# Half of a branch's gated product kept on chip, loads issued in another order, a smaller DMA scratch

## The chip, the cores and the metric

The program runs on one core of a Trainium2 chip. The core has a matrix engine (TensorE, PE in the profile; its weight loads are PEld), a vector engine (VectorE, DVE), a scalar engine (ScalarE, ACT), a general engine (GpSimd, POOL) and a sync engine (SyncE, SP) that issues transfers. Each engine takes its own instructions in order and waits on semaphores for the others; transfers run on 16 DMA engines. The metric is the device time of one execution, in microseconds, and the median of several executions.

## What is computed

A bidirectional encoder of two layers on one sequence of 512 tokens with 1024 channels, in float32. Cut to what matters:

```python
for l in range(DEPTH):                                   # DEPTH = 2
    xn = rms_norm(x, ln1[l])
    z = xn @ w_in[l]                                     # one projection for all branches
    a_q, a_i, a_ff, a_fb, a_g, b_u, b_v, c_q, c_k, c_v, gz = jnp.split(z, offsets, axis=-1)
    o_a = hgrn2_bidirectional(a_q, a_i, a_ff, a_fb, lower[l])         # branch A, 4 heads
    y_a = rms_norm(o_a, a_norm[l]) * jax.nn.silu(a_g)
    y_b = spatial_gating(jax.nn.gelu(b_u), jax.nn.gelu(b_v), w_s[l], b_s[l])
    y_c = window_attention(rope(c_q), rope(c_k), c_v, sink[l])        # branch C, 8 query heads
    gates = jax.nn.sigmoid(gz.reshape(bsz, s_len, N_BRANCH, D_MODEL))
    merged = (gates[:, :, 0] * (y_a @ w_br[l, 0])
              + gates[:, :, 1] * (y_b @ w_br[l, 1])
              + gates[:, :, 2] * (y_c @ w_br[l, 2]))
    x = x + merged @ w_out[l]
    x = x + jnp.square(jax.nn.relu(rms_norm(x, ln2[l]) @ w_up[l])) @ w_down[l]
return rms_norm(x, final_norm)
```

The change touches the last of the three products in `merged` and what follows it up to the residual.

## The kernel before

**Tiles and precision.** Activations are held as tiles of 128 partitions by 512 values (256 KB). A float32 product is made of three matmuls in a reduced format: every operand is split in a high part (a cast on ScalarE, L207 for weights, L270 for activations) and a low part (a subtraction on VectorE, L208 and L271), and the matmuls are high by high, high by low, and low by high. `proj_tok` (L262 to L264) does this for the projections of the branches with tokens on the partitions: four PSUM tiles, one for each 128 tokens, and half of the 1024 output channels at a time (`fl` is 0 or 1). Weights come through SyncE's queue into `wr` and are split into `wh` and `wl`.

**Order.** The code is written layer by layer. A scheduler puts the instructions of each engine in an order, from the code, its priorities (`later(...)` pushes work back, `hp()` brings it forward) and its own estimate of durations. Tiles come from tags with a fixed number of slots (the table SLOTS); a new tile of a tag waits until the users of the slot's earlier tile are done. At run time each engine keeps its order.

**Stages of a layer around the change.** Branch A's heads run one after the other in `a_head` (L581 to L669). The end of a head is a chain: scores `at` (TensorE, from `qt` and `kt` made by ScalarE), transposes `kT` and their copy (L624, L626), states `stp` and `st` (L629, L636), the product `av` (L652), squares and sums `asq` (ScalarE, L657), `ms` and `rs` (VectorE and GpSimd, L280, L282), the scaled `ao` (VectorE, L660) and transposes `oT` (TensorE, L664). Between its steps stands other work: branch C's attention (scores L972, transposed weights `pT` L1001 and their copy L1002, output `po` L1006, copies to `yc` L1008) and branch C's projection `yC`.

Branch C's gated product (L1054 to L1063): for each half, `gates` loads four tiles `th` from DRAM (tag `ch` here), `yC` is projected, VectorE forms (th + 1) * yC in place, and the tile is stored to the DRAM buffer `mcd`. Both halves go there. Then branch A's four outputs are gated and split into `yh` and `yl` (L1066 and `split`); `yh` takes tag `tv`. That tag has eight slots: earlier in the layer they hold branch A's four value tiles `vt`, branch C's keys `k2` and the low parts of the keys `kl` (two each).

The merge (L1090 to L1106): for each half, loads of `th` and of the four `mC` tiles back from `mcd` (tag `mg`), the projection `yA`, VectorE's (th + 1) * yA at L1101 and the sum into `mC` at L1102. `turn_sum` transposes `mC` to `mT` on TensorE (L1081), loads branch B's part `mB` from DRAM (`mgd`), adds (L1086) and splits the result into `mgh` and `mgl`, the operands of the output projection `wo`. The PSUM tag of the first half's `mT` has two buffers. Then the residual `xr` is loaded (eight tiles, tag `l`, L1111), and `wo` is projected and added to it (L1117).

All loads and stores named here are issued by GpSimd, in its order; an issue waits until the GpSimd transfer eight before it has landed, since their semaphores are used in turn. In layer 0 that order is: eight stores to `mcd`, four `xr`, four `th`, four `mC`, four `mB`, four `mC`, then the other `xr` mixed with the second half's `th`, and the second half's `mB`.

Of the kernel before, what the change touches and what calls it, by code (L numbers as in the profile page):

```python
# [6 lines left out]
F32 = mybir.dt.float32  # L7
# [3 lines left out]
ALU = mybir.AluOpType  # L11

P = 128
S = 512
# [46 lines left out]
def trunk(tc, xT, xt, ws, vec, fnb, bsb, snk, wst, rope, cmask, amask, ident, out):  # L61
    nc = tc.nc
# [3 lines left out]
    def pool(**kw):  # L66
        p = tc.tile_pool(**kw)
        pools.append(p)
        return p.__enter__()
# [6 lines left out]
    dram = pool(name="dram", bufs=1, space=bass.MemoryType.DRAM)  # L76
# [4 lines left out]
             "xs": 16, "zt": 6,  # L81
             "yh": 8,
             "q": 2, "a": 3, "g": 2, "ch": 10,
             "yi": 16, "th": 8, "mg": 8,
             "h": 22}

    HOME = {t: p for p, ts in {"G": ("xs", "zt"), "Y1": ("yh",), "br": ("q", "a", "g", "ch"), "Y2": ("yi", "th", "mg"), "mlp": ("h",)}.items() for t in ts}
# [5 lines left out]
    def nm(s):  # L93
        ctr[0] += 1
        return f"{s}_{ctr[0]}"

    def T(tag, name, dt=F32):
        where = part[HOME[tag]] if tag in HOME else sb
        return where.tile([P, S], dt, tag=tag, bufs=SLOTS[tag], name=nm(name))
# [33 lines left out]
    def hp():  # L133

        return tc.high_priority() if boost[0] else contextlib.nullcontext()
# [562 lines left out]
    for i in range(8):  # L698
        t = T("tv", "xt")
# [5 lines left out]
    xsrc = xt  # L705
    xspill = dram.tile([P, 4, D], F32, name="xspill")
    thd = dram.tile([P, 8, D], F32, name="thd")
    mgd = dram.tile([P, KT, S], F32, name="mgd")
    mcd = dram.tile([P, 8, S], F32, name="mcd")

    for l in range(DEPTH):
        xs = n1.xs
# [176 lines left out]
        def y_split(ys, tag):  # L889
            res = []  # L890
            for y in ys:
                hi, lo = T(tag, "yh", F32R), T(tag, "yl", F32R)
                split(y, hi, lo)
                res.append((hi, lo))
            return res
# [19 lines left out]
        def gate_a():  # L915
            z = evac(proj(xs, "ag", l, "ag", len(sg)), "l2", "ag")
            th = T("jk", "th")
            nc.scalar.activation(th, z, AF.Tanh, scale=0.5)
            nc.vector.scalar_tensor_tensor(z, th, 1.0, z, ALU.add, ALU.mult)
            sg.append(z)  # L920
# [131 lines left out]
        with later(30000):  # L1052
            for h in range(4):
                gate_a()  # L1054

            ys = y_split(yc, "yh")
            for fl in range(2):
                th = gates("ch", 0, fl)
                pts = proj_tok(ys, "yC", (l, "y", 2, fl), 0)
                for t in range(4):  # L1060
                    with hp():
                        nc.vector.scalar_tensor_tensor(th[t], th[t], 1.0, pts[t], ALU.add, ALU.mult)
                    nc.gpsimd.dma_start(mcd[:, fl * 4 + t], th[t])  # L1063
        ys = []
        for h in range(4):
            nc.vector.scalar_tensor_tensor(oa[h], oa[h], 0.5, sg[h], ALU.mult, ALU.mult)  # L1066
# [23 lines left out]
        ms = [None] * KT  # L1090
        for fl in range(2):
            th = gates("th", 1, fl)
            mc = []
            for t in range(4):
                m = T("mg", "mC")
                nc.gpsimd.dma_start(m, mcd[:, fl * 4 + t])
                mc.append(m)
            pts = proj_tok(ys, "yA", (l, "y", 0, fl), fl)
            for t in range(4):
                with hp():  # L1100
                    nc.vector.scalar_tensor_tensor(th[t], th[t], 1.0, pts[t], ALU.add, ALU.mult)  # L1101
                    nc.vector.tensor_tensor(mc[t], mc[t], th[t], ALU.add)  # L1102
            mcs.append(mc)
            if fl == 0:
                turn_sum(0)


        xr = [[T("l", "xr"), T("l", "xr")] for _ in range(4)]
        for fl in range(2):
            for t in range(4):  # L1110
                nc.gpsimd.dma_start(xr[t][fl], xsrc[:, t, fl * S:(fl + 1) * S])  # L1111
        n2 = norm_tok("ln2", l, xr, False)
        for fl in range(2):
            pts = proj_tok(ms, "wo", (l, "wo", fl), fl, None if fl else lambda: turn_sum(1))
# [103 lines left out]
        xsrc = xspill  # L1218
# [121 lines left out]
```

## Time and profile before

| | before |
|---|---|
| runs, us | 1723.64, 1722.11, 1719.17; median 1722.11 |
| profiled execution, us | 1720.54, of which the recorded span is 1718.7 |
| mean granted TensorE clock | 0.997 |
| DMA moved | 200.04 MB, mean 116 GB/s |
| transfers issued by GpSimd | 166 of 256 KB or less |

The profiled execution lies 1.57 us below the median of the runs and 1.84 us above its span. The table of granted clock by slices holds a 9 throughout, so the clock is the same in all stages. In the rows of the trace the first number is the start in us from the span's start, the second the duration in us, then engine, line, operation, output and inputs; brackets hold the idle time of the engine before the row and what ended it. A matmul's recorded duration overlaps the next one: what a train of them costs is read from the distance of their starts.

### The profile page before, as it was taken

The page shows a single profiled execution, that of the slowest core. Times are in us where ns is not written, and L with a number is a line of the kernel's source. Part 1 is how long each engine was busy: PE and PEld are TensorE (multiplying, and loading weights), DVE is VectorE, ACT ScalarE, POOL GpSimd, SP SyncE. Part 2 cuts the span into 40 slices and gives each one's busy share as a digit, 9 for nine tenths or more (in the row PEclk, how much of TensorE's full clock was granted, in tenths as well). Part 3 has the DMA queues.
Part 4 walks back from the last instruction along what each step waited for, and adds up shares of the span by engine and source line. Part 5 has one row for each costly group of instructions (what it writes and reads, how often), then busy time and mean ns, then how long its engine had stood idle before and what let it go on. Part 6 is the DMA issues. An engine that isn't in the chain of part 4 may idle for free.

```text
span 1718.7 us, 21970 instructions
## 1 busy us (share of the span) xinstructions
PE 1679.9 (98%) x8024; PEld 1402.0 (82%) x8024; DVE 1296.1 (75%) x2009; ACT 1016.7 (59%) x1715; POOL 146.3 (9%) x215
## 2 busy tenths in 40 slices
PE   8999989999999999999999999999999999999997
PEld 7888878888778888888888787888878788888886
DVE  7996977687566768686889869876875667585967
ACT  7665567676335555545665754877872355545464
POOL 0011200000310000000010112000004000000001
PEclk9999999999999999999999999999999999999999
DMA  8342232231555332322323422322316453232311
GB/s 333 98 147 92 84 105 75 80 105 55 189 204 183 104 105 98 98 98 98 135 88 127 153 91 74 104 69 86 104 56 246 158 184 99 98 103 94 123 62 49
DMA packets 58283, 200.04 MB, mean 116 GB/s; under 512 B 7904, under 2 KB 8288, under 8 KB 58176
## 3 DMA queue, kind: packets, MB, share of 16 engines
q1 hardware_dynamic: 44640, 154.72, 26.8%
q0 software_dynamic: 13248, 43.40, 6.8%
q8 instruction: 63, 1.03, 0.2%
q10 hardware_dynamic: 288, 0.52, 0.1%
q14 instruction: 44, 0.36, 0.1%
HBM read 177.64 MB, written 20.97 MB: 116 GB/s over the span
## 4 chain that ended last, share of the span: by engine, by line
PE 61%; issue 25%; DVE 8%; ACT 4%; POOL 1%; DMA 1%; POOLq 0%; SPq 0%; DVEq 0%; ACTq 0%
PE up L212 3%; PE up L214 3%; PE up L213 3%; PE at L567 2%; PE dA L427 2%; PE dA L429 2%; PE wo L264 2%; PE dA L428 2%; PE wo L263 2%; PE po L1006 2%; PE gz L214 2%; PE gz L212 2%; PE gz L213 2%; PE wo L262 2%; DVE ex L609 1%
## 5 line engine op out<-in xcount | busy, mean ns | idle before, releaser
L207 ACT CAST wh<-wq 128x1024 fp32r<-128x1024 f32 x201 | 211.5, 1053 | 205.1 <-PE up L213 47.4
L208 DVE TENSOR_TENSOR wl<-wq,wh 128x1024 fp32r<-128x1024 f32 x201 | 244.8, 1220 | 113.1 <-ACT wh L207 112.1
L208 DVE TENSOR_TENSOR wl<-wr,wh 128x1024 fp32r<-128x1024 f32 x166 | 203.7, 1227 | 145.4 <-ACT wh L207 145.0
L207 ACT CAST wh<-wr 128x1024 fp32r<-128x1024 f32 x166 | 174.2, 1049 | 222.8 <-PE up L213 75.0
L212 PE MATMUL up<-xh,wh 128*128 128x512 f32 x512 | 199.3, 389 | 0.0
L213 PE MATMUL up<-xl,wh 128*128 128x512 f32 x512 | 199.2, 389 | 0.0
L214 PE MATMUL up<-xh,wl 128*128 128x512 f32 x512 | 198.2, 389 | 0.0
L214 PEld LDWEIGHTS up<-xh,wl 128*128 128x128 f32 x512 | 96.1, 188 | 20.0
L212 PEld LDWEIGHTS up<-xh,wh 128*128 128x128 f32 x512 | 96.1, 188 | 19.9
L213 PEld LDWEIGHTS up<-xl,wh 128*128 128x128 f32 x512 | 96.1, 188 | 19.8
L427 PE MATMUL dA<-wh,sh 128*128 128x512 f32 x256 | 99.7, 389 | 0.0
L428 PE MATMUL dA<-wh,sh 128*128 128x512 f32 x256 | 99.6, 389 | 0.0
L429 PE MATMUL dA<-wl,sh 128*128 128x512 f32 x256 | 92.6, 389 | 0.0
L609 DVE TENSOR_TENSOR ex<-ex 128x512 f32<-128x512 f32 x112 | 78.0, 714 | 6.3 <-ACT kt L584 5.6
L567 PEld LDWEIGHTS at<-qt,kt 128*128 128x128 f32 x448 | 57.0, 191 | 10.0 <-ACT kt L584 4.7
L567 PE MATMUL at<-qt,kt 128*128 128x128 f32 x448 | 59.6, 276 | 5.6 <-DVE qt L582 2.7
L581 ACT ACTIVATE qt<-ex 128x512 f32<-128x512 f32 x56 | 37.8, 674 | 45.9 <-DVE ex L609 38.3
L282 POOL TENSOR_TENSOR rs<-ms,mhalf_t 128x4 f32<-128x4 f32 (+2 forms) x15 | 17.3, 1156 | 524.6 <-DVE ms L280 521.5
L427 PEld LDWEIGHTS dA<-wh,sh 128*128 128x128 f32 x256 | 48.1, 188 | 10.0
L429 PEld LDWEIGHTS dA<-wl,sh 128*128 128x128 f32 x256 | 48.1, 188 | 10.0
L428 PEld LDWEIGHTS dA<-wh,sh 128*128 128x128 f32 x256 | 48.1, 188 | 9.9
L270 ACT CAST sh<-sf 128x512 fp32r<-128x512 f32 x64 | 39.6, 619 | 21.9 <-DVE sf L392 16.7
(403 smaller groups left out, 4393.2 us busy)
## 6 DMA issues: line engine op xcount, KB each, us to landing
wr<-in_ws_dram SPq DMA_DIRECT2D x166, 512.0 KB, 3.3
wq<-in_ws_dram SPq DMA_DIRECT2D x117, 512.0 KB, 4.3
thd<-zt POOLq DMA_DIRECT2D x32, 256.0 KB, 2.4
th<-thd POOLq DMA_DIRECT2D x32, 256.0 KB, 5.2
mgd<-mg POOLq DMA_DIRECT2D x16, 256.0 KB, 2.9
mcd<-th POOLq DMA_DIRECT2D x16, 256.0 KB, 2.5
mC<-mcd POOLq DMA_DIRECT2D x16, 256.0 KB, 6.7
mB<-mgd POOLq DMA_DIRECT2D x16, 256.0 KB, 5.9
```

What stands on the lines that cost most here:

```text
L207: nc.scalar.copy(hi, raw)
L208: nc.vector.tensor_tensor(lo, raw, hi.bitcast(F32), ALU.subtract)
L212: nc.tensor.matmul(pt, whi, xhi, start=first, stop=False)
L213: nc.tensor.matmul(pt, whi, xlo, start=False, stop=False)
L214: return nc.tensor.matmul(pt, wlo, xhi, start=False, stop=last)
L270: nc.scalar.copy(hi, src)
L427: nc.tensor.matmul(pt, xh[:, t], hi[:, c], start=start and k == 0, stop=False, skip_group_check=True)
L428: nc.tensor.matmul(pt, xl[:, t], hi[:, c], start=False, stop=False, skip_group_check=True)
L429: nc.tensor.matmul(pt, xh[:, t], lo[:, c], start=False, stop=k == 3, skip_group_check=True)
L567: nc.tensor.matmul(pt[:, c], kk(st), qq[:, c], start=True, stop=True)
L581: nc.scalar.activation(qt.rearrange(shp, b=nb, h=2), e_q, AF.Exp)
L609: nc.vector.tensor_tensor(o_ap, o_ap, ap_of(ex, i_, [[istep, 2]] + z), ALU.add)
```

## The change

Three edits. The first half (`fl` = 0) of branch C's gated product is written to four new tiles of tag `tv`, kept there until the merge, and neither stored nor loaded; `mcd` holds four tiles and tag `mg` four slots. The residual loads are ordered behind the last `mC` load by `issue_after`. The scratch memory for GpSimd's transfers is set to 4096 bytes, from a default of 16384.

```diff
--- before.py
+++ after.py
@@ -81,7 +81,7 @@
              "xs": 16, "zt": 6,
              "yh": 8,
              "q": 2, "a": 3, "g": 2, "ch": 10,
-             "yi": 16, "th": 8, "mg": 8,
+             "yi": 16, "th": 8, "mg": 4,
              "h": 22}
 
     HOME = {t: p for p, ts in {"G": ("xs", "zt"), "Y1": ("yh",), "br": ("q", "a", "g", "ch"), "Y2": ("yi", "th", "mg"), "mlp": ("h",)}.items() for t in ts}
@@ -706,7 +706,7 @@
     xspill = dram.tile([P, 4, D], F32, name="xspill")
     thd = dram.tile([P, 8, D], F32, name="thd")
     mgd = dram.tile([P, KT, S], F32, name="mgd")
-    mcd = dram.tile([P, 8, S], F32, name="mcd")
+    mcd = dram.tile([P, 4, S], F32, name="mcd")
 
     for l in range(DEPTH):
         xs = n1.xs
@@ -1054,13 +1054,18 @@
                 gate_a()
 
             ys = y_split(yc, "yh")
+            kept = []
             for fl in range(2):
                 th = gates("ch", 0, fl)
                 pts = proj_tok(ys, "yC", (l, "y", 2, fl), 0)
                 for t in range(4):
+                    if fl == 0:
+                        kept.append(T("tv", "mC"))
+                    m = th[t] if fl else kept[t]
                     with hp():
-                        nc.vector.scalar_tensor_tensor(th[t], th[t], 1.0, pts[t], ALU.add, ALU.mult)
-                    nc.gpsimd.dma_start(mcd[:, fl * 4 + t], th[t])
+                        nc.vector.scalar_tensor_tensor(m, th[t], 1.0, pts[t], ALU.add, ALU.mult)
+                    if fl:
+                        nc.gpsimd.dma_start(mcd[:, t], m)
         ys = []
         for h in range(4):
             nc.vector.scalar_tensor_tensor(oa[h], oa[h], 0.5, sg[h], ALU.mult, ALU.mult)
@@ -1090,11 +1095,10 @@
         ms = [None] * KT
         for fl in range(2):
             th = gates("th", 1, fl)
-            mc = []
-            for t in range(4):
-                m = T("mg", "mC")
-                nc.gpsimd.dma_start(m, mcd[:, fl * 4 + t])
-                mc.append(m)
+            mc = kept if fl == 0 else [T("mg", "mC") for _ in range(4)]
+            if fl:
+                for t in range(4):
+                    ld = nc.gpsimd.dma_start(mc[t], mcd[:, t])
             pts = proj_tok(ys, "yA", (l, "y", 0, fl), fl)
             for t in range(4):
                 with hp():
@@ -1108,7 +1112,8 @@
         xr = [[T("l", "xr"), T("l", "xr")] for _ in range(4)]
         for fl in range(2):
             for t in range(4):
-                nc.gpsimd.dma_start(xr[t][fl], xsrc[:, t, fl * S:(fl + 1) * S])
+                with tc.issue_after(ld.ins):
+                    nc.gpsimd.dma_start(xr[t][fl], xsrc[:, t, fl * S:(fl + 1) * S])
         n2 = norm_tok("ln2", l, xr, False)
         for fl in range(2):
             pts = proj_tok(ms, "wo", (l, "wo", fl), fl, None if fl else lambda: turn_sum(1))
@@ -1324,7 +1329,7 @@
     import concourse.tile as _tile
     from concourse.bass_utils import run_bass_kernel_spmd as _run
 
-    nc = _bacc.Bacc("TRN2", target_bir_lowering=False, num_devices=1)
+    nc = _bacc.Bacc("TRN2", target_bir_lowering=False, num_devices=1, dynamic_dma_scratch_size=4096)
     host = _host(**{k: np.asarray(v) for k, v in inputs.items()})
     arrays, args = {}, []
     for name in _NAMES:
```

The number of instructions of TensorE, VectorE, ScalarE and SyncE is the same as before, and so is SyncE's order. GpSimd issues 150 transfers in place of 166. What changes place lies in both layers between the end of head 3 and the first part of the output projection. The three places below are word for word from the order of each engine; numbers at the ends of names differ by eight between the two programs from here on.

**First: layer 0, the end of head 3.** TensorE before: the last `yC` matmuls and the transposes `oT`. The nine rows of `av` that end the head stand 34 wide matmuls ahead of the first of these.

```order
L264 MATMUL yC_4116<-wl_4152,yh_4023 128x512
L262 MATMUL yC_4117<-wh_4151,yh_4023 128x512
L263 MATMUL yC_4117<-wh_4151,yl_4024 128x512
L264 MATMUL yC_4117<-wl_4152,yh_4023 128x512
L664 MATMUL oT_3704<-id_t,ao_3702 128x128 x4
L262 MATMUL yC_4118<-wh_4151,yh_4023 128x512
L263 MATMUL yC_4118<-wh_4151,yl_4024 128x512
L264 MATMUL yC_4118<-wl_4152,yh_4023 128x512
L262 MATMUL yA_4228<-wh_4233,yh_4188 128x512
```

TensorE with the change: the end of `av`, then `oT`.

```order
L652 MATMUL av_3681<-st_3655,qd_3659 128x128
L652 MATMUL av_3681<-st_3674,qd_3678 128x128
L652 MATMUL av_3681<-vt_653,at_3534 128x128
L652 MATMUL av_3681<-st_3655,qd_3659 128x128
L664 MATMUL oT_3704<-id_t,ao_3702 128x128 x4
L262 MATMUL yA_4355<-wh_4361,yh_4188 128x512
L262 MATMUL yA_4356<-wh_4361,yh_4188 128x512
L263 MATMUL yA_4219<-wh_4225,yl_4189 128x512
L264 MATMUL yA_4219<-wl_4226,yh_4188 128x512
L263 MATMUL yA_4220<-wh_4225,yl_4189 128x512
L264 MATMUL yA_4220<-wl_4226,yh_4188 128x512
```

ScalarE before, where the first two casts of branch A's `yh` stand (the third follows ten rows on): in the middle of branch C's attention.

```order
L1002 COPY pT_2769<-pT_2770 128x2x128
L270 CAST yh_4019<-yc_2606 128x512
L581 ACTIVATE qt_3571<-ex_3492 128x512
L270 CAST yh_4188<-on_1565 128x512
L270 CAST yh_4193<-on_2373 128x512
L1002 COPY pT_2769<-pT_2774 128x2x128
L979 ACTIVATE sc_2789,su_2784<-sc_2789,mx_2783 128x384
```

ScalarE with the change: all three behind the last copy of `kT` (L626) and ahead of `asq`.

```order
L638 ACTIVATE qd_3678<-ex_3492 128x384
L207 CAST wh_4255<-wr_4253 128x1024
L626 COPY kT_3668<-kT_3664 128x384
L207 CAST wh_4361<-wr_4359 128x1024
L270 CAST yh_4188<-on_1565 128x512
L270 CAST yh_4193<-on_2373 128x512
L270 CAST yh_4198<-on_3319 128x512
L657 ACTIVATE asq_3692,ss_3693<-av_3681 128x128 x4
L666 ACTIVATE on_3709<-oT_3704,vec_t 128x512
L270 CAST yh_4203<-on_3709 128x512
```

The `yC` matmuls that stood between `av` and `oT` now stand earlier, 12 of them ahead of the last scores (L567) and 44 ahead of `stp`; and the casts of `yh` wait for `av`, whose operand `vt` held their slots: `yh_4188` for the first `av` row, the next two for later ones. The first `po` of the stretch's last pair stands ahead of the scores that it stood behind.

**Second: layer 0, the merge, VectorE.** Before: the sums into `mC`, the `mB` adds and the first low part.

```order
L1102 TENSOR_TENSOR mC_4223<-mC_4223,th_4215 128x512
L1102 TENSOR_TENSOR mC_4225<-mC_4225,th_4217 128x512
L1086 TENSOR_TENSOR mB_4306<-mB_4306,mT_4299 128x512
L1086 TENSOR_TENSOR mB_4318<-mB_4318,mT_4311 128x512
L208 TENSOR_TENSOR wl_4567<-wr_4564,wh_4566 128x1024
L1086 TENSOR_TENSOR mB_4330<-mB_4330,mT_4323 128x512
L271 TENSOR_TENSOR mgl_4305<-mB_4306,mgh_4304 128x512
L1086 TENSOR_TENSOR mB_4342<-mB_4342,mT_4335 128x512
L271 TENSOR_TENSOR mgl_4317<-mB_4318,mgh_4316 128x512
```

With the change:

```order
L1106 TENSOR_TENSOR mC_4105<-mC_4105,th_4217 128x512
L208 TENSOR_TENSOR wl_4481<-wr_4478,wh_4480 128x1024
L1105 SCALAR_TENSOR_TENSOR th_4339<-th_4339,yA_4355 128x512
L1106 TENSOR_TENSOR mC_4347<-mC_4347,th_4339 128x512
L1105 SCALAR_TENSOR_TENSOR th_4341<-th_4341,yA_4356 128x512
L1091 TENSOR_TENSOR mB_4298<-mB_4298,mT_4291 128x512
L1091 TENSOR_TENSOR mB_4310<-mB_4310,mT_4303 128x512
L1106 TENSOR_TENSOR mC_4348<-mC_4348,th_4341 128x512
L1105 SCALAR_TENSOR_TENSOR th_4343<-th_4343,yA_4357 128x512
L208 TENSOR_TENSOR wl_4559<-wr_4556,wh_4558 128x1024
L1091 TENSOR_TENSOR mB_4322<-mB_4322,mT_4315 128x512
L271 TENSOR_TENSOR mgl_4297<-mB_4298,mgh_4296 128x512
```

Three instructions of the second half (`th_4339`, `mC_4347`, `th_4341`) now stand ahead of the first `mB` add, two more ahead of the first `mgl`.

**Third: layer 1, the merge, TensorE.** Before: the last rows of the projection `yA` and the transposes of the first half; the eight rows from `mT_11623` on come next.

```order
L264 MATMUL yA_11665<-wl_11700,yh_11503 128x512
L1081 MATMUL mT_11599<-id_t,mC_11521 128x128
L1081 MATMUL mT_11611<-id_t,mC_11521 128x128
L262 MATMUL yA_11666<-wh_11699,yh_11503 128x512
L263 MATMUL yA_11666<-wh_11699,yl_11504 128x512
L264 MATMUL yA_11666<-wl_11700,yh_11503 128x512
L1081 MATMUL mT_11599<-id_t,mC_11523 128x128
L1081 MATMUL mT_11611<-id_t,mC_11523 128x128
L1081 MATMUL mT_11599<-id_t,mC_11525 128x128
L1081 MATMUL mT_11611<-id_t,mC_11525 128x128
L1081 MATMUL mT_11623<-id_t,mC_11519 128x128
```

With the change: the last of the first two `mT` stand nine `yA` matmuls ahead of the next transposes.

```order
L264 MATMUL yA_11647<-wl_11684,yh_11495 128x512
L1086 MATMUL mT_11583<-id_t,mC_11397 128x128
L1086 MATMUL mT_11595<-id_t,mC_11397 128x128
L262 MATMUL yA_11648<-wh_11683,yh_11495 128x512
L263 MATMUL yA_11648<-wh_11683,yl_11496 128x512
L264 MATMUL yA_11648<-wl_11684,yh_11495 128x512
L262 MATMUL yA_11649<-wh_11683,yh_11495 128x512
L263 MATMUL yA_11649<-wh_11683,yl_11496 128x512
L264 MATMUL yA_11649<-wl_11684,yh_11495 128x512
L262 MATMUL yA_11650<-wh_11683,yh_11495 128x512
L263 MATMUL yA_11650<-wh_11683,yl_11496 128x512
L264 MATMUL yA_11650<-wl_11684,yh_11495 128x512
```

The transposes of the first two tiles have moved up into `yA`; on VectorE the first two `mB` adds keep their place behind the last `mC` sum. In layer 1's end of head 3 the transposes `kT` have moved from ahead of the last `po` to behind it, and another `po` ahead of nine `yC` matmuls; the 34 matmuls between `av` and `oT` stay there too.

On GpSimd, layer 0 now has: four stores to `mcd`, four `th`, four `mB`, four `mC`, four `xr`, then the second half's `th` mixed with the other `xr`, and the second half's `mB`.

## What I predict

> **What bounds the kernel now.** I read the page first (busy shares and the chain of waits), then busy time by stretch, then the waits of TensorE in the stretches that the change reorders, then single rows.
>
> ```profile
> PE 1679.9 (98%) x8024; PEld 1402.0 (82%) x8024; DVE 1296.1 (75%) x2009; ACT 1016.7 (59%) x1715; POOL 146.3 (9%) x215
> ...
> PE 61%; issue 25%; DVE 8%; ACT 4%; POOL 1%; DMA 1%; POOLq 0%; SPq 0%; DVEq 0%; ACTq 0%
> ```
>
> TensorE is busy for 98% of the span, and DMA carries 1% of the chain that ended last. The change takes no instruction from TensorE. So it can only win or lose idle time of TensorE, and only where instructions change places: from the end of head 3 to the output projection, once in each layer. The view of busy time by stretch shows how much idle time is there (columns: stretch, then busy us of PE, PEld, DVE, ACT and POOL with counts, clock, DMA share).
>
> ```profile
> 412.00:440.00 28.00, 22.41 (x138) 19.07 (x137) 20.80 (x49) 20.96 (x56) 0.00 (x0) 1.00 0.08 29
> ...
> 453.00:470.00 17.00, 17.00 (x79) 14.00 (x78) 9.71 (x15) 4.36 (x5) 9.75 (x19) 1.00 0.86 318
> 470.00:500.00 30.00, 28.48 (x137) 22.44 (x136) 22.65 (x34) 9.09 (x12) 9.08 (x17) 1.00 0.70 265
> 1266.00:1303.00 37.00, 33.43 (x195) 28.62 (x195) 25.84 (x56) 23.64 (x65) 4.35 (x7) 1.00 0.24 86
> ...
> 1320.00:1352.00 32.00, 30.48 (x146) 24.09 (x145) 25.04 (x37) 10.04 (x13) 10.25 (x20) 1.00 0.77 298
> ```
>
> TensorE idles 5.6 us before head 3's end in layer 0, 1.5 in layer 0's merge, 3.6 and 1.5 in the same places of layer 1: 12.2 us, 0.7% of the span. No order could gain more here. Where the DMA share is 0.86 (453 to 470), TensorE is busy for 17.00 of 17.00 us: the loads that the change removes stand beside a full TensorE.
>
> **The transfers.** Removed per layer: 4 stores to `mcd` and 4 loads from it. The rows are, in this order, the page's list of DMA issues (count, size, median us from issue to landing), one issue on POOL, one wait of VectorE, and the tile view of the residuals (minimum, median and maximum ns, first and last start).
>
> ```profile
> th<-thd POOLq DMA_DIRECT2D x32, 256.0 KB, 5.2
> ...
> mcd<-th POOLq DMA_DIRECT2D x16, 256.0 KB, 2.5
> mC<-mcd POOLq DMA_DIRECT2D x16, 256.0 KB, 6.7
> ```
> ```profile
> 464.02 0.54 POOL L1096 DMA_DIRECT2D mC<-mcd  x1 [1.41 <-DMA xr<-in_xt_dram]
> ```
> ```profile
> 467.04 1.28 DVE L1101 SCALAR_TENSOR_TENSOR th<-th,yA 128x512 f32<-128x512 f32 x2 [2.91 <-DMA th<-thd]
> ```
> ```profile
> L1117 DVE SCALAR_TENSOR_TENSOR xr<-wo,xr x16: 691/692/693, 505.0 to 1381.6; 128x512 f32<-128x512 f32 x16
> ...
> L1111 POOL DMA_DIRECT2D xr<-in_xt_dram x8: 536/538/543, 457.0 to 480.6; - x8
> ```
>
> 16 issues of 0.54 us leave POOL, 8.6 us in all, on an engine that is busy 9%: worth nothing. The load of `mC` waits 1.41 us for residual loads issued before it, and VectorE waits 2.91 us for `th`. Both go when the residual loads move behind the merge's loads, but both end inside 453 to 470, where TensorE has no idle time: nothing again. The residuals are issued a few us later than now; the last of layer 0 is issued at 480.6 now and the first is read at 505.0, so this costs nothing either. Behind the residuals on POOL stand the second half's `th` loads, as now. The multiply that now writes a kept tile has the same shape as before: nothing.
>
> **Layer 0, end of head 3.** These are TensorE's waits between 412 and 441 (us in total, times, longest).
>
> ```profile
> PE at L567 <- ACT kt L584: 2.0, 2, 1.8
> PE stp L629 <- ACT kT L626: 1.8, 1, 1.8
> PE po L1006 <- ACT pT L1002: 1.4, 1, 1.4
> PE at L567 <- ACT sc L988: 0.4, 1, 0.4
> PE yC L263 <- DVE yl L271: 0.3, 1, 0.3
> ```
>
> That is 5.9 us now. In the new order 12 matmuls of `yC` stand behind the last scores and 44 in all before `stp`, so the waits for `kt` and `kT` (1.8 each) vanish. But the same matmuls are then missing further on. First row group: the chain behind the last `av`, and what covers it now. Second: ScalarE's casts of branch A's first three heads, and rows for the price of moving `po` ahead.
>
> ```profile
> 444.91 0.39 PE L652 MATMUL av<-st,qd 128*128 128x128 f32 x2
> ...
> 445.33 0.28 ACT L657 ACTIVATE asq<-av 128x128 f32<-128x128 f32 x1 [4.15 <-PE av L652]
> ...
> 446.83 1.03 POOL L282 TENSOR_TENSOR rs<-ms,mhalf_t 128x4 f32<-128x4 f32 x1 [1.98 <-DVE ms L280]
> ...
> 447.90 0.69 DVE L660 TENSOR_TENSOR ao<-av,rs 128x512 f32<-128x512 f32 x1 [1.22 <-POOL rs L282]
> ...
> 452.67 0.40 PE L264 MATMUL yC<-wl,yh 128*128 128x512 f32 x1
> ...
> 452.90 0.60 PE L664 MATMUL oT<-id_t,ao 128*128 128x128 f32 x4
> ```
> ```profile
> 411.65 1.12 ACT L270 CAST yh<-on 128x512 fp32r<-128x512 f32 x2
> ...
> 428.96 0.37 ACT L1002 COPY pT<-pT 128x256 f32<-128x256 f32 x1
> 429.23 0.63 ACT L581 ACTIVATE qt<-ex 128x512 f32<-128x512 f32 x1
> ...
> 430.82 0.63 ACT L584 ACTIVATE kt<-ex 128x512 f32<-128x512 f32 x1
> ```
> ```profile
> 429.31 0.38 PE L1001 MATMUL pT<-id_t,sc 128*128 128x128 f32 x2
> ```
>
> - `av` ends at 445.3, `ao` at 448.6, and `oT` needs `ao`. Now 34 wide matmuls at 0.23 us (452.67 to 452.90) stand between; in the new order none. **3.3 us** of idle time appear.
> - Branch A's `yh` tiles share their slots with `vt`, `k2` and `kl`. So far the casts run early, two of them at 411.65, in slots of the keys. In the new order those hold `mC`, so the first cast waits for the first `av` matmul, and the next TensorE row reads it. One cast of 0.56 us (1.12 for two) and two handovers: **0.7 us**. Behind it on ScalarE stand two more such casts and the four `asq`; they wait for later `av` anyway, and are in the 3.3.
> - `po` stands ahead of the next scores; it needs a `pT` copy that ScalarE makes behind `qt` and `kt`. Counted from 428.96 that is a copy, `qt`, `kt` and a copy, 0.27 + 0.63 + 0.63 + 0.37, so about 430.8; TensorE is free at 429.7 (429.31 + 0.38): **1.1 us**. If `kt` stays at its 430.82, it is 2.2.
> - The 12 `yC` matmuls need the cast of the last `yc`, behind two copies on ScalarE: about **0.5 us** (an estimate from the 0.62 us of a cast).
>
> With the 1.4 us for `pT` and the 0.4 for `sc` that stay: 1.4 + 0.4 + 1.1 + 0.5 + 0.7 + 3.3 = 7.4 against 5.9: **+1.5 us**. Ends: -1.0 (neither wait for `pT` is left) and +4.0 (the old waits stay, and 0.7 and 3.3 come on top).
>
> **Layer 0, merge.** 1.5 us of idle now, here and in layer 1 with the same rows; layer 1's are shown below. In the new order three instructions of the second half stand on VectorE ahead of the first `mB` add.
>
> ```profile
> 476.63 1.28 DVE L1086 TENSOR_TENSOR mB<-mB,mT 128x512 f32<-128x512 f32 x2 [2.27 <-PE mT L1081]
> ```
>
> At 0.64 each they delay the add by 1.9 us at most, but it waits 2.27 for TensorE now, so most of that is free. I take **-0.2**, since the second half's adds are done earlier. Ends: -2.1 (all gone, as in layer 1) and +1.9.
>
> **Layer 1, end of head 3.** Here the order is nearly that of before; `kT` moves from ahead of a waiting `po` to behind it.
>
> ```profile
> 1285.72 0.53 PE L624 MATMUL kT<-id_t,kd 128*128 128x128 f32 x3
> 1287.95 1.13 PE L1006 MATMUL po<-pT,cvt 128*128 128x256 f32 x4 [1.70 <-ACT pT L1002]
> 1288.92 0.83 PE L629 MATMUL stp<-vt,kT 128*128 128x128 f32 x6
> ```
>
> Now the `kT` transposes and their copy lie in the 1.70 us. Behind `po` they stand open: `kT` at 1288.92, 0.53 us, a copy of about 0.4 (as `pT`'s above, an estimate), so `stp` at 1289.9 in place of 1288.92: **+1.0**. Ends: 0, and +2.0 for nine `yC` matmuls at 0.23 that another `po` now stands ahead of.
>
> **Layer 1, merge.** The last eight transposes of `mT` need a PSUM slot that the first `mB` add frees.
>
> ```profile
> 1329.87 0.60 PE L1081 MATMUL mT<-id_t,mC 128*128 128x128 f32 x4
> 1331.14 1.25 PE L1081 MATMUL mT<-id_t,mC 128*128 128x128 f32 x8 [0.67 <-DVE mB L1086]
> 1332.15 0.71 PE L262 MATMUL wo<-wh,mgh 128*128 128x512 f32 x2
> 1333.47 0.50 PE L262 MATMUL wo<-wh,mgh 128*128 128x512 f32 x1 [0.61 <-DVE mB L1086]
> 1334.07 0.50 PE L263 MATMUL wo<-wh,mgl 128*128 128x512 f32 x1
> ```
>
> A transpose issues every 0.11 us, a wide matmul every 0.23: the gaps are 1.27 - 0.44, 1.32 - 0.46 and 0.60 - 0.23, together 2.1 us. In the new order the last of the first `mT` transposes stand nine wide matmuls (2.1 us) ahead of the eight, since `mC` is at hand; two adds of 0.64 and a cast fit in that. **-2.1**; ends -2.1 and 0.
>
> **Sum.** +1.5 - 0.2 + 1.0 - 2.1 = +0.2 us, ends -5.2 and +7.9. The profiled execution took 1720.54 us, 1.57 below the median of the three runs (1722.11, of 1719.17 to 1723.64); +0.2 on the median gives **1722.3**. What a measurement of this kernel can tell from no change is about 0.3%, 5.2 us: I forecast no difference that shows.
>
> **The smaller scratch.** No row prices it. At most eight POOL transfers are in flight (an issue waits for the one eight before it), and issues take 0.54 us throughout, so nothing here looks short of room. [...]
>
> **Rivals.**
> - *Both merges and the end of head 3 fall to the good ends* (the reordering covers more than it opens): -1.0 - 2.1 - 2.1 = -5.2, with no loss in layer 1: 1716.9 us. For it: 12.2 us of idle time are there; against: nothing stands between the last `av` and `oT`. Chance 0.10.
> - *The uncovered end of head 3 decides, slower*: `yh` waits for `vt`, `av` to `oT` stands open (+4.0 in layer 0), `po` moves into a wait in layer 1 (+2.0), and the merges gain nothing: +6.0, 1728.1 us. It decides once the waits for `kt` and `kT` do not vanish. Chance 0.12.
> - *The smaller scratch holds POOL's transfers back.* In layer 1 the merge's loads begin at
>
> ```profile
> 1313.24 2.12 POOL L1015 DMA_DIRECT2D th<-thd  x4
> ```
>
> and the first `wo` at 1332.15, 19 us later. With a quarter of the transfers in flight (two), the 12 loads that the merge needs first, at some 5.9 us (the middle of the 5.2 and 6.7 above), take 12 / 2 x 5.9 = 35 us: +16 per layer, 1754 us. Against it stands the even issue time. Chance 0.04.
> - *The change does nothing on the path*, the round trip having been hidden: 1722.1 us, inside my forecast's range.
>
> **How the numbers follow.** Forecast 0.74 (1718.5 to 1725.5, the last rival in it). Faster by over 0.3% (below 1716.9): half of the first rival and a little of the forecast's edge, 0.06. Slower (above 1727.3): most of the second, the third, and an edge, 0.12. Within: 0.82. The range 1717.0 to 1727.5 leaves out about half of each of the first two rivals, and the third.
>
> **What would show it.** In layer 0, TensorE idle for some 3.3 us ahead of `oT`, put down to `ao`, and a wait for `yh` of about 0.7 at the first `yA`; the waits of `at` for `kt` and of `stp` for `kT` gone. In layer 1, no wait of `mT` or `wo` for `mB`, and `stp` behind `kT` by about 1 us. VectorE's wait for `th` (2.91) gone with no change in TensorE's 453 to 470. Issue times on POOL at 0.54. I am wrong if TensorE's idle time in these stretches moves by more than 5 us in sum, or if POOL's issues grow.

## The result, and the profile after

| | before | changed |
|---|---|---|
| median, us (14 runs each) | 1721.22 | 1723.84 |
| span of the profiled execution, us | 1718.7 | 1721.4 |
| ratio to before | | 1.0017, 95% interval 1.001 to 1.0025 |

The change makes the kernel slower by 2.6 us, 0.17%: less than the 0.3% that I had put as the bound, but clear of noise. The page of the changed kernel hardly differs from that of before (engines' busy time; then the shares of the chain that ended last):

```profile
PE 1680.9 (98%) x8024; PEld 1403.1 (82%) x8024; DVE 1296.9 (75%) x2009; ACT 1016.2 (59%) x1715; POOL 137.2 (8%) x199
...
PE 59%; issue 25%; DVE 7%; ACT 5%; DMA 2%; POOL 1%; SPq 0%; POOLq 0%; DVEq 0%; ACTq 0%
```

GpSimd lost 9 us of work, and the shares of the chain show nothing of it. Where the time went is seen by following the same matmul in both traces. These are rows of the tile views of `oT` and `up` (minimum, median, maximum ns, then the first and the last start): first the kernel before, then the changed one.

```profile
L664 PE MATMUL oT<-id_t,ao x32: 270/272/275, 266.2 to 1307.0; 128*128 128x128 f32 x32
```
```profile
L212 PE MATMUL up<-xh,wh x512: 389/389/476, 527.6 to 1671.3; 128*128 128x512 f32 x171
```
```profile
L664 PE MATMUL oT<-id_t,ao x32: 270/272/327, 267.2 to 1313.5; 128*128 128x128 f32 x32
```
```profile
L212 PE MATMUL up<-xh,wh x512: 389/389/476, 532.8 to 1675.2; 128*128 128x512 f32 x171
```

The first `oT` (head 0, layer 0, long before anything is reordered) stands 1.0 us later, which belongs to no part of the change. The first `up`, behind layer 0's merge, stands 5.2 us later, so layer 0 costs 5.2 - 1.0 = **4.2 us**. The last `up`, behind layer 1, stands 3.9 later. Between the layers another 0.4 us came in around 1025 us, where no instruction has moved; from 1240 to 1400 us the shift falls from 5.5 to 3.9, so layer 1 gains **1.6 us**. 4.2 - 1.6 = 2.6 us, which is the difference of the medians. In the profiled execution the rest nearly cancels: 1.0 us at the start, 0.4 between the layers, and -1.3 at the very end, where behind the last stores of the output the shift falls from 3.9 to 2.6.

The stretches of the prediction, in the changed kernel (busy time of PE, PEld, DVE, ACT and POOL with counts, granted clock, DMA share):

```profile
412.00:440.00 28.00, 24.85 (x141) 21.03 (x140) 23.35 (x48) 20.12 (x52) 0.56 (x2) 1.00 0.11 31
...
453.00:470.00 17.00, 13.31 (x57) 10.55 (x56) 5.83 (x9) 3.82 (x12) 9.45 (x17) 0.90 0.61 206
470.00:500.00 30.00, 27.39 (x132) 21.45 (x132) 22.23 (x33) 9.00 (x12) 6.60 (x13) 1.00 0.64 224
1266.00:1303.00 37.00, 31.99 (x191) 27.67 (x190) 28.69 (x62) 25.75 (x66) 0.61 (x1) 1.00 0.11 37
...
1320.00:1352.00 32.00, 31.92 (x155) 26.29 (x155) 23.17 (x33) 9.38 (x11) 14.96 (x28) 1.00 0.87 326
```

Ahead of head 3's end TensorE idles less (3.2 us instead of 5.6), in layer 1's merge not at all (0.1 instead of 1.5). But 453 to 470, where it never waited, now holds 3.7 us of idle time, and a clock of 0.90. Layer 0's tail, row by row on TensorE (start, duration, brackets with idle time and its releaser):

```profile
429.69 1.13 PE L1006 MATMUL po<-pT,cvt 128*128 128x256 f32 x4 [1.00 <-ACT pT L1002]
...
449.88 1.68 PE L262 MATMUL yA<-wh,yh 128*128 128x512 f32 x6 [0.71 <-ACT yh L270]
...
456.90 0.66 PE L664 MATMUL oT<-id_t,ao 128*128 128x128 f32 x4 [3.34 <-DVE ao L660]
457.31 0.67 PE L262 MATMUL yA<-wh,yh 128*128 128x512 f32 x1
458.34 0.80 PE L262 MATMUL yA<-wh,yh 128*128 128x512 f32 x1 [0.35 <-ACT on L666]
458.93 0.63 PE L263 MATMUL yA<-wh,yl 128*128 128x512 f32 x1
459.36 0.63 PE L264 MATMUL yA<-wl,yh 128*128 128x512 f32 x1
459.78 0.63 PE L263 MATMUL yA<-wh,yl 128*128 128x512 f32 x1
460.21 0.63 PE L264 MATMUL yA<-wl,yh 128*128 128x512 f32 x1
460.64 0.49 PE L263 MATMUL yA<-wh,yl 128*128 128x512 f32 x1
460.97 0.40 PE L264 MATMUL yA<-wl,yh 128*128 128x512 f32 x1
461.20 0.39 PE L263 MATMUL yA<-wh,yl 128*128 128x512 f32 x1
```

The three predicted waits stand where they were expected, at 1.00, 0.71 and 3.34 us. Behind the 3.34 comes something that was not: wide matmuls 0.43 us apart (458.93, 459.36, 459.78, 460.21) until about 460.9, then 0.23 again. The view of short stretches names the cause; its clock column reads 0.50 from 457.43 to 460.84 us and 1.00 on both sides:

```profile
454.02:457.43 3.41, 0.53 (x5) 0.53 (x5) 1.45 (x4) 0.72 (x6) 1.03 (x1) 1.00 0.00 0
457.43:460.84 3.41, 3.06 (x9) 2.07 (x8) 2.51 (x5) 1.31 (x2) 2.74 (x6) 0.50 0.37 120
460.84:464.26 3.42, 3.42 (x16) 2.81 (x16) 0.00 (x0) 0.00 (x0) 3.16 (x6) 1.00 0.86 274
```

From 458.34 to 461.20 seven matmuls take 2.86 us in place of 1.6, and the one at 457.31 takes 0.45 more than its 0.23 and the wait behind it: about **1.7 us** lost to the clock. The sizes agree with the clock column: 0.43 us is about twice 0.23, and the stretch at 0.50 lasts 3.41 us. The 3.41 us ahead of the fall held five matmuls, 0.53 us of work; in run 7 below TensorE was busy for 1.72 of the 3.42 us ahead of it, half of the time.

Layer 0's merge in the changed kernel, TensorE and then ScalarE:

```profile
481.32 1.26 PE L1086 MATMUL mT<-id_t,mC 128*128 128x128 f32 x8 [0.41 <-DVE mB L1091]
483.85 0.73 PE L262 MATMUL wo<-wh,mgh 128*128 128x512 f32 x2 [1.27 <-ACT mgh L270]
...
485.19 0.50 PE L262 MATMUL wo<-wh,mgh 128*128 128x512 f32 x1 [0.38 <-DVE mB L1091]
...
497.42 0.66 PE L1086 MATMUL mT<-id_t,mC 128*128 128x128 f32 x4 [0.45 <-DVE mB L1091]
```
```profile
482.23 1.05 ACT L207 CAST wh<-wr 128x1024 fp32r<-128x1024 f32 x1 [6.71 <-DMA wr<-in_ws_dram]
483.18 1.14 ACT L270 CAST mgh<-mB 128x512 fp32r<-128x512 f32 x2
```

TensorE waits four times, 2.5 us in all, where it waited twice, 1.3 us, before. The largest wait is for `mgh`, whose cast stands behind a weight cast on ScalarE that had waited for its weights. VectorE's wait of 2.9 us for `th` ahead of the merge's first product is one of 1.3 us for a load now. Layer 1 has waits ahead of head 3's end (us in total, times, longest) and none in the merge:

```profile
PE at L567 <- ACT kt L584: 1.8, 1, 1.8
PE stp L629 <- ACT kT L626: 1.8, 1, 1.8
PE po L1006 <- ACT pT L1002: 1.5, 1, 1.5
```

### The profile page after: what moved, and what is told of

It reads as the page before. It is cut to its first block, busy times and chain, and to the rows that moved or that the text cites. A ratio compares the mean times of both kernels' runs of the same rounds, so it can differ in the third digit from the quotient of the medians.

```text
span 1721.4 us, 21946 instructions
## 1 busy us (share of the span) xinstructions
PE 1680.9 (98%) x8024; PEld 1403.1 (82%) x8024; DVE 1296.9 (75%) x2009; ACT 1016.2 (59%) x1715; POOL 137.2 (8%) x199
## 3 DMA queue, kind: packets, MB, share of 16 engines
q8 instruction: 63, 1.03, 0.2%
## 4 chain that ended last, share of the span: by engine, by line
PE 59%; issue 25%; DVE 7%; ACT 5%; DMA 2%; POOL 1%; SPq 0%; POOLq 0%; DVEq 0%; ACTq 0%
PE up L214 3%; PE up L213 3%; PE up L212 3%; PE at L567 2%; PE wo L263 2%; PE dA L429 2%; PE dA L428 2%; PE dA L427 2%; PE wo L264 2%; PE wo L262 2%; PE po L1006 2%; PE gz L214 2%; PE gz L212 2%; PE gz L213 2%; DVE ex L609 1%
## 5 line engine op out<-in xcount | busy, mean ns | idle before, releaser
L567 PEld LDWEIGHTS at<-qt,kt 128*128 128x128 f32 x448 | 57.1, 191 | 7.2 <-ACT kt L584 2.6
L567 PE MATMUL at<-qt,kt 128*128 128x128 f32 x448 | 59.3, 275 | 3.4 <-ACT kt L584 1.8
```

Source lines behind the costliest of these rows:

```text
L567: nc.tensor.matmul(pt[:, c], kk(st), qq[:, c], start=True, stop=True)
```

## The experiments

My theory for the loss was that of the slots: the kept tiles take the slots in which branch A's first casts `yh` were made early; `yh` must then wait for `vt`, which frees its slots only with the last product `av` of head 3, and the order that the scheduler makes around this leaves head 3's end uncovered. The rivals were the smaller scratch, the order of the residual loads, and contention of loads. The last two columns give by how much each layer moved against the kernel before, from the shift of the same ScalarE instructions (medians over 20 us at 380 and at 540 us, at 1240 and at 1400 us). The kernel before ran beside each group: its medians were 1721.46 us beside runs 1 to 4, 1721.78 beside 5, 6, 7 and 9, and 1721.94 beside 8. The layer columns stand on one profiled execution of each kernel; those of runs 6 and 7 were the slowest executions of their kernels and that of 8 the second slowest, so there the columns come out worse than the medians.

| kernel | median us (runs) | ratio to before, interval | layer 0 | layer 1 |
|---|---|---|---|---|
| the change | 1723.84 (14) | 1.0017, 1.001 to 1.0025 | +4.2 | -1.6 |
| scratch only | 1719.89 (11) | 0.9993, 0.9984 to 1.0001 | +0.1 | 0.0 |
| residual order only | 1719.95 (11) | 0.9991, 0.9982 to 1.0000 | -0.8 | -0.8 |
| change without residual order | 1724.80 (11) | 1.0018, 1.0009 to 1.0026 | +5.1 | -1.7 |
| kept tiles in slots of their own | 1714.71 (5) | 0.9959, 0.9947 to 0.9971 | -2.6 | -2.6 |
| that, without residual order | 1715.83 (5) | 0.9967, 0.9953 to 0.9980 | -2.7 | -2.7 |
| `yh` in slots of its own | 1715.31 (5) | 0.9963, 0.9950 to 0.9976 | -0.4 | -2.9 |
| gap filled, 20 transposes | 1724.50 (11) | 1.0017, 1.0008 to 1.0026 | +7.7 | -1.6 |
| gap filled, 10 wide matmuls | 1724.81 (11) | 1.0014, 1.0005 to 1.0023 | +6.8 | -1.7 |
| residual loads last | 1724.69 (10) | 1.0016, 1.0007 to 1.0025 | +4.3 | -1.2 |

**1. The scratch alone.**

```diff
-    nc = _bacc.Bacc("TRN2", target_bir_lowering=False, num_devices=1)
+    nc = _bacc.Bacc("TRN2", target_bir_lowering=False, num_devices=1, dynamic_dma_scratch_size=4096)
```

> The kernel before, with only the scratch memory for GpSimd's transfers set to 4096 bytes; the order of every engine is that of before. Slot theory (the loss comes from branch A's yh tiles having to wait for the slots of vt): 0 us, within 1 us of before, issues on GpSimd at 0.54 us. Scratch theory (the smaller scratch holds transfers back): about +2.6 us, the whole loss of the change, with longer issues or landings on GpSimd's queue.

Within noise of before, and both layers unmoved. The scratch is out. The tile view of `mcd` also shows issues as short as before (median 540 ns, where the kernel before has 542):

```profile
L1063 POOL DMA_DIRECT2D mcd<-th x16: 539/540/605, 441.6 to 1311.3; - x16
```

**2. The residual order alone**, with both halves still going through DRAM.

```diff
-                nc.gpsimd.dma_start(m, mcd[:, fl * 4 + t])
+                ld = nc.gpsimd.dma_start(m, mcd[:, fl * 4 + t])
...
-                nc.gpsimd.dma_start(xr[t][fl], xsrc[:, t, fl * S:(fl + 1) * S])
+                with tc.issue_after(ld.ins):
+                    nc.gpsimd.dma_start(xr[t][fl], xsrc[:, t, fl * S:(fl + 1) * S])
```

> The kernel before, with only the residual loads ordered behind the last mC load; both halves still go through DRAM. Slot theory: the end of head 3 keeps the order of before, so no idle time of 3.3 us ahead of oT and no loss there; within 2 us of before. Theory that the order of the loads does the damage (residual loads landing together with the output projection's weights): slower by 1 to 3 us, with ScalarE waiting several us for a weight tile in the merge. Theory that the order of the loads brings the merge's gain: faster by 4 to 5 us.

0.8 us less in each layer by the profile; the interval of the runs ends at 1.0000. The order of the loads neither does the damage nor brings the 4 to 5 us that its rival asked for.

**3. The change without the residual order.**

```diff
-                with tc.issue_after(ld.ins):
-                    nc.gpsimd.dma_start(xr[t][fl], xsrc[:, t, fl * S:(fl + 1) * S])
+                nc.gpsimd.dma_start(xr[t][fl], xsrc[:, t, fl * S:(fl + 1) * S])
```

> The changed kernel without the ordering of the residual loads. In layer 0 the order of all engines is that of the changed kernel; in layer 1 the merge's order differs. Slot theory: layer 0 loses its 4.2 us as before, so about +2.6 us on the kernel before, with at most 1 us either way from layer 1's merge. Theory that the ordering of the residuals brings layer 1's gain of 2.5 us: about +5 us.

As slow as the change, and layer 1 gains 1.7 us where the change gained 1.6. So neither the loss nor the gain hangs on the residual loads. Layer 0, whose order is the same as in the change, lost 5.1 instead of 4.2 us here: the clock stayed at half for twice as long, from 455.71 to 462.54 us, where the change had 457.43 to 460.84.

```profile
455.71:459.13 3.42, 2.00 (x6) 1.49 (x7) 2.97 (x5) 0.69 (x1) 0.98 (x3) 0.50 0.00 0
459.13:462.54 3.41, 3.41 (x9) 2.64 (x9) 0.91 (x2) 0.62 (x1) 3.41 (x7) 0.50 0.72 232
```

**4. Slots of their own for the kept tiles.** The four slots take 8 KB more of each partition.

```diff
-    SLOTS = {"x": 16, "l": 8, "l2": 4, "tv": 8, "rb": 1, "jk": 1,
+    SLOTS = {"x": 16, "l": 8, "l2": 4, "tv": 8, "mk": 4, "rb": 1, "jk": 1,
...
-                        kept.append(T("tv", "mC"))
+                        kept.append(T("mk", "mC"))
```

> The changed kernel with the four kept tiles in slots of their own, so that branch A's yh can again take the slots of branch C's keys. All engines keep the order of before up to the merge in both layers; both merges have the order that layer 1's merge has in the changed kernel. Slot theory: no idle time ahead of oT, no wait for yh, and 2.1 to 2.5 us gained in each merge: 4 to 5 us faster than before (about 1716.5 us), 7 faster than the change. Rival (the loss is due to the loads, the scratch or to keeping the tiles at all): still 2 to 3 us slower than before.

1714.71 us, 6.8 us below the 1721.46 us of the runs of before beside it: faster than both kernels, and more than the 4 to 5 us that I had written (the profile accounts for 5.2 of it; the interval is 5 to 9). In its stretches the idle time that head 3 had before is back, 453 to 470 is full again at a clock of 1.00, and the merges are full:

```profile
412.00:440.00 28.00, 22.02 (x135) 18.74 (x135) 20.80 (x48) 21.75 (x57) 0.31 (x1) 1.00 0.09 29
...
453.00:470.00 17.00, 17.00 (x78) 13.94 (x77) 11.45 (x17) 4.36 (x5) 8.04 (x15) 1.00 0.70 230
470.00:500.00 30.00, 29.92 (x148) 24.62 (x147) 21.75 (x31) 8.96 (x12) 8.59 (x16) 1.00 0.73 282
...
1320.00:1352.00 32.00, 31.92 (x157) 26.26 (x156) 22.10 (x32) 9.60 (x13) 8.81 (x17) 1.00 0.70 272
```

This settles the cause of the loss: the same transfers removed, the same residual order, the same scratch, and only the tag of four tiles changed, with the order of the engines that follows from it.

**5. The same without the residual order** (edit as in 3).

> The kernel with slots of their own for the kept tiles, without the ordering of the residual loads. Slot theory: 0.5 to 2 us slower than with it (1715 to 1717 us), still 4 us faster than before, since keeping the tiles carries most of the merges' gain. Rival (the ordering of the residual loads carries most of it): 3 us or more slower than with it, within 2 us of before.

Both layers gain 2.7 us, as much as with it; the medians differ by 1.1 us with intervals that overlap. Keeping the tiles carries the merges' gain; with it the residual order is worth nothing that these runs show.

**6. Slots of its own for `yh`**, the kept tiles staying in the keys' slots.

```diff
-    SLOTS = {"x": 16, "l": 8, "l2": 4, "tv": 8, "rb": 1, "jk": 1,
+    SLOTS = {"x": 16, "l": 8, "l2": 4, "tv": 8, "ya": 4, "rb": 1, "jk": 1,
...
-            hi, lo = T("tv", "yh", F32R), T("l", "yl", F32R)
+            hi, lo = T("ya", "yh", F32R), T("l", "yl", F32R)
```

> The changed kernel with the kept tiles in the slots of the keys, as the change has them, and branch A's yh in four slots of its own. Slot theory (it is yh that loses by the sharing, not the kept tiles): no wait for yh, no idle time of 3.3 us ahead of oT, and as fast as with slots of their own for the kept tiles, 1714 to 1717 us. Rival (the kept tiles themselves come late, since they wait for the keys' last readers): slower than that by 3 us or more, with VectorE's product waiting and yC short of PSUM.

1715.31 us: either side of the sharing may move out. In the profiled execution, the slowest of the five (1718.20 us), layer 0 gained only 0.4 us, and the clock was low here too: its mean is 0.58 from 430 to 436 us and 0.50 from 436 to 441, behind 6 us at 1.00 in which TensorE was busy for 4.24. What this cost was not measured.

```profile
424.00:430.00 6.00, 4.24 (x29) 3.38 (x27) 5.09 (x9) 3.55 (x10) 0.00 (x0) 1.00 0.25 87
430.00:436.00 6.00, 4.10 (x15) 3.55 (x15) 2.46 (x4) 4.65 (x14) 0.00 (x0) 0.58 0.00 0
436.00:441.00 5.00, 4.43 (x17) 3.76 (x16) 2.06 (x5) 2.11 (x5) 0.00 (x0) 0.50 0.02 5
```

**7. The gap filled with transposes.** These add work whose output is overwritten.

```diff
-                nc.tensor.matmul(po[:, c], w_, m_, start=i == 0, stop=i == len(parts) - 1)
+                av = nc.tensor.matmul(po[:, c], w_, m_, start=i == 0, stop=i == len(parts) - 1)
...
         pt = PT("a", "oT")
+        if l == 0 and h == 3:
+            with tc.issue_after(av.ins):
+                for i in range(20):
+                    c = slice(i % 4 * P, (i % 4 + 1) * P)
+                    nc.tensor.transpose(pt[:, c], q[:, c], id_t)
```

> The changed kernel with 20 additional transposes of a ready tile on TensorE between the last av and oT of layer 0's head 3 (2.2 us of work; oT overwrites what they write). Clock theory (TensorE's clock is lowered after 3.3 us of idle time, and its next matmuls take 0.43 us in place of 0.23): oT stands as late as without them, the granted clock behind it is 1.00, the first yA matmuls issue every 0.23 us, and 1.5 to 2 us are won on the changed kernel in this place. Rival (the slow matmuls behind oT come from their own waits, for weights or for yl): they still issue at about 0.43 us, no gain. The order of layer 0's merge moves a little too, by up to 1 us either way, so the place is read, not only the total.

A miss, in the place and in the total. The idle time ahead of `oT` shrank to 1.16 us, yet the clock from 458.67 to 462.08 was 0.50, with nine matmuls in these 3.41 us, where the change at 1.00 had 16 in 3.42 (460.84 to 464.26). So the clock fell with 1.16 us of idle time ahead of `oT` as with 3.34.

```profile
457.01 0.66 PE L669 MATMUL oT<-id_t,ao 128*128 128x128 f32 x4 [1.16 <-DVE ao L660]
```
```profile
455.25:458.67 3.42, 1.72 (x12) 1.17 (x11) 2.40 (x4) 0.69 (x1) 1.44 (x2) 1.00 0.00 0
458.67:462.08 3.41, 3.41 (x9) 2.65 (x9) 1.39 (x3) 0.62 (x1) 3.41 (x8) 0.50 0.71 216
```

**8. The gap filled with wide matmuls**, the order of every engine otherwise that of 7.

```diff
-                for i in range(20):
-                    c = slice(i % 4 * P, (i % 4 + 1) * P)
-                    nc.tensor.transpose(pt[:, c], q[:, c], id_t)
+                for i in range(10):
+                    nc.tensor.matmul(pt, n1.xs[0][0][:, :P], n1.xs[0][1], start=True, stop=True)
```

> As the kernel with the gap filled by 20 transposes, with ten matmuls of 128x512 in their place (also 2.2 us; oT overwrites what they write); the order of every engine is otherwise the same. Theory (transposes and narrow products don't hold the clock up, wide matmuls do): the granted clock behind oT is 1.00, the first yA matmuls issue every 0.23 us, the second slow stretch in the merge goes as well or shrinks, and this kernel is 1.5 to 4 us faster than the one with transposes. Rival (any idle time of about 1 us at this place, or the low load of the av products ahead of it, lowers the clock): matmuls behind oT still issue every 0.43 us, same time.

Now the clock holds, and the matmuls behind `oT` come 0.24 us apart, with 1.03 us of idle time ahead of `oT`. The view of stretches, then the rows:

```profile
454.27:457.69 3.42, 2.39 (x12) 1.64 (x12) 1.24 (x3) 0.93 (x8) 1.03 (x1) 1.00 0.03 12
457.69:461.10 3.41, 2.86 (x15) 2.14 (x13) 2.72 (x5) 1.31 (x2) 2.53 (x5) 1.00 0.33 89
```
```profile
457.37 0.66 PE L668 MATMUL oT<-id_t,ao 128*128 128x128 f32 x4 [1.03 <-DVE ao L660]
...
459.14 0.40 PE L263 MATMUL yA<-wh,yl 128*128 128x512 f32 x1
459.38 0.40 PE L264 MATMUL yA<-wl,yh 128*128 128x512 f32 x1
```

That does not show that wide matmuls hold the clock up and transposes do not. The two fillers also differ in how busy they kept TensorE and when: in the 3.42 us ahead of the fall (455.25 to 458.67) it was busy for 1.72 us with the transposes, and in the 3.42 us from 454.27 to 457.69, behind which the clock held, for 2.39 us with the wide matmuls. The kind of the work, its place and its amount changed together, and no run here separates them.

From `oT` to the first group of four high-by-high matmuls (461.01) it takes 3.6 us; with transposes 5.2, in the change 4.8. In the total nothing is left of it: in the order that both filled kernels share, the first `wo` of layer 0's merge waits 2.9 us here and 1.8 with transposes for `mgh`, where the change had 1.27. So the clock held in this place, as expected; why is open, and the expected gain in time did not come.

**9. The residual loads last**, behind the last `mB` load.

```diff
-                nc.gpsimd.dma_start(m, mgd[:, d])
+                lb.append(nc.gpsimd.dma_start(m, mgd[:, d]))
...
-                with tc.issue_after(ld.ins):
-                    nc.gpsimd.dma_start(xr[t][fl], xsrc[:, t, fl * S:(fl + 1) * S])
...
+            if fl == 0:
+                for f in range(2):
+                    for t in range(4):
+                        with tc.issue_after(lb[-1].ins):
+                            nc.gpsimd.dma_start(xr[t][f], xsrc[:, t, f * S:(f + 1) * S])
```

> The changed kernel with the residual loads behind the last mB load. Theory of contention (in layer 0's merge a weight tile of the output projection takes 7.3 us to land because residual loads run beside it, ScalarE waits for it, and the first wo behind it): the tile lands in 5 us or less, the wait ahead of the first wo shrinks by about 1 us, layer 0 costs about 3 us in place of 4.2. Rival (the wait comes from the order of VectorE and ScalarE): the wait stays at 1.3 us.

Half a hit. The weight tiles of this stretch land in 4.4 us (median of three) where the change had 7.2 with the residuals beside them, first this kernel, then the change:

```profile
wr<-in_ws_dram SPq DMA_DIRECT2D x3, 512.0 KB, 4.4
```
```profile
wr<-in_ws_dram SPq DMA_DIRECT2D x3, 512.0 KB, 7.2
```

The first `wo` no longer waits for its cast. But the next one waits 1.3 us for an `mB` add, which stands behind six instructions of the second half on VectorE, and layer 0 costs 4.3 us, as much as in the change (4.2). The contention shows in these loads and is not what bounds the merge; VectorE's order is next in line, which no run tested.

Not tried: both halves kept on chip, which would take eight slots; and the same filler at another time ahead of `oT`.

## Why the prediction was right, and what it missed

The measured time lies in my range, and "no difference of 0.3%" was right. "No difference that shows" was not: with 14 runs of each, 2.6 us show. That the total came so near owes something to luck: layer 0 came out 2.9 us worse than my +1.3, and layer 1 0.5 us better than my -1.1. The working held in most steps:

- *The transfers are worth nothing*: right. Runs 3 to 5 show gain and loss to depend on slots and on where `mC` is, not on the order of the loads; the smaller scratch did nothing (run 1). Keeping the tiles pays through the order of the merge, 2.7 us in each layer in run 5, not through the bytes.
- *Layer 0, end of head 3, +1.5*: the single waits came out at 1.4, 1.0, 0.4, 0.7 and 3.3 us against 1.4, 1.1, 0.5, 0.7 and 3.3 in the sum. The wait for `sc` that I kept is gone, one of 0.4 for `yl` stayed. Together 7.2 against 5.9: +1.3.
- *Layer 1, end of head 3, +1.0*: the shift is +0.9. `stp` waits for `kT`, as said, but for 1.8 us and not 1.0; and the wait for `kt` grew from 0.5 to 1.8, which was not in my working, while waits of 1.1 (`qt`) and 0.3 (`yh`) went. In waits the place came out at 5.1 against 3.6 us, so the near hit is partly luck.
- *Layer 1, merge, -2.1*: -2.6 by the shift (6.5 to 3.9), a little beyond my good end of -2.1; no wait left.

Two terms were missed, both in layer 0. Together they come to some 3.4 us; with what layer 1 gained beyond my working, and 0.2 in the waits ahead of `oT`, that leaves roughly the 2.4 us between my +0.2 and the 2.6 measured:

- *The gap ahead of `oT` cost more than its length.* My step priced it at 3.3 us of idle time and let the matmuls behind run at 0.23 us. They ran at 0.43 for 3.4 us: 1.7 us more, and a wait of 0.35 for `on`. The kernel before held the warning. In its layer 1 two waits of 1.6 and 2.0 us lie close together, and the row behind them has a clock of 0.63 (by the trace 0.50 from 1077.57 to 1080.98 us). So the clock before was not the same in all stages, as I had read from the page: in a slice of 43 us, 3.4 us at half clock still leave 0.96, a 9.

```profile
1071.00:1076.70 5.70, 2.13 (x15) 1.69 (x13) 5.57 (x10) 2.00 (x5) 0.00 (x0) 1.00 0.00 0
1076.70:1080.00 3.30, 3.27 (x9) 2.60 (x10) 3.24 (x5) 1.24 (x4) 0.00 (x0) 0.63 0.32 99
```

- *Layer 0's merge, -0.2*, came out at +1.2 in waits. I had three instructions of the second half ahead of the first `mB` add and called most of it free. The first add was indeed little later; but the first cast `mgh` waits behind a weight tile that landed late, and the third add and the first low part behind two more. Without the late tile (run 9) the wait moved to the third add. The bounds (-2.1 and +1.9) held, the value was on the wrong side.

The rival "the uncovered end of head 3 decides, slower" named the right place and the right mechanism; its condition (the waits for `kt` and `kT` stay) did not occur in layer 0, and its price of 6 us was too high, since layer 1's merge gained as forecast. The third rival's two transfers in flight are an assumption that no run shows: in the trace of the changed kernel, with a scratch of 4096 bytes, up to eight GpSimd transfers are between issue and landing, as many as before.

## What to carry to other kernels

A tile that is kept on chip to save a load that was hidden anyway is paid for by whoever wanted its slots: look up who takes the slots of that tag next, when they were free before and when they will be now. A wait on the matrix engine is to be priced with what follows it: in the profiled execution the 3.34 us ahead of `oT` were followed by 3.41 us at a clock of 0.50, which cost another 1.7 us; a wait of 2.91 us in the kernel before (at 218.74 us) was followed by a clock of 1.00. And where order and storage change together, give the new tiles slots of their own once: that alone turned 0.17% slower into 0.41% faster.

## What the runs showed of the hardware

- Between 30 and 1700 us the matrix engine's granted clock is 1.00 or 0.50 in the traces of the kernel before and of the change. It reads 0.50 from 1077.57 to 1080.98 us before, and from 457.43 to 460.84 and from 1082.07 to 1085.48 us in the change: 3.41 us each. In these stretches wide matmuls in a train come 0.43 us apart, against 0.23 at 1.00. In run 3 the clock is 0.50 from 455.71 to 462.54, 6.83 us.
- Ahead of a fall TensorE was busy, by the records of its matmuls, for 1.39 of 3.41 us before, 0.53 and 1.13 of 3.41 in the change, 0.67 of 3.41 in run 1 and 1.72 of 3.42 in run 7. The length of a single wait does not go with the fall by itself. The kernel before waits 2.91 us ahead of the matmul at 218.74 us, and the clock stays at 1.00. In the one with the smaller scratch alone, which has the same order, 3.41 us with 0.67 us of matmuls (217.54 to 220.95) are followed by 3.41 us at 0.50. What decides between the two is not shown. First two stretches of the kernel before, then two of run 1:

```profile
214.00:217.41 3.41, 1.83 (x10) 1.41 (x8) 3.25 (x6) 2.65 (x4) 0.00 (x0) 1.00 0.00 0
217.41:220.83 3.42, 2.09 (x9) 1.74 (x10) 3.39 (x5) 0.04 (x1) 0.00 (x0) 1.00 0.02 2
```
```profile
217.54:220.95 3.41, 0.67 (x3) 0.58 (x4) 3.35 (x5) 1.45 (x2) 0.00 (x0) 1.00 0.00 0
220.95:224.36 3.41, 3.41 (x10) 2.63 (x9) 3.35 (x6) 0.26 (x1) 0.00 (x0) 0.50 0.47 159
```

- With the same order in layer 0, the slow stretch behind `oT` ended at about 460.9 us in the change and at about 462.5 in run 3. The runs of the change spread over 5.9 us, the five with slots of their own over 1.1. In the change, the four runs with a mean granted clock of 0.993 took 1724.27 to 1727.78 us, the ten others 1721.92 to 1724.59. The clock goes with the spread; that it makes it was not tested.
- A 512 KB load of weights took 4.4 us to land with the residual loads out of the way and 7.2 beside them (medians of three loads in layer 0's merge).
